# A macaron decoder trunk on one core: another order of the feed-forwards' first products, earlier convolution taps, own tiles for residual sums, a split last tile

## The chip, the cores and the metric

The kernel runs on 1 core of one Trainium2 chip. The metric is the device time of one execution in microseconds (us); where runs are compared, it is the median of several. Engines are named as in the profile: PE (TensorE, matmuls and transposes), PEld (its weight loads), DVE (VectorE), ACT (ScalarE), POOL (GpSimd), SP (SyncE, which issues nearly all DMAs).

## The reference

One layer over 1024 tokens of width 1024, in float32:

```python
x = x + 0.5 * swiglu(rms_norm(x, ffn1_norm), w_gate, w_up, w_down)      # hidden width 2816
x = x + token_mixer(rms_norm(x, mix_norm) @ w_in) @ w_out
x = x + 0.5 * swiglu(rms_norm(x, ffn2_norm), w_gate2, w_up2, w_down2)
out = rms_norm(x, final_norm)

def swiglu(h, w_gate, w_up, w_down):
    return (silu(h @ w_gate) * (h @ w_up)) @ w_down
```

The token mixer joins three parts along the channels: a pool mixer (256 channels: trailing means over 2, 4, 8 and 16 tokens minus the token, then a small matrix per group), attention with forget gates (8 heads of 64; the logits get the running sum of the log gates) and a convolution part (256 channels: a gated linear unit, a causal depthwise convolution of 31 taps, a layer norm, silu). All matrices are multiplied to float32 accuracy.

## The kernel before, in words

**Precision.** Each operand is split into a high and a low part: ACT casts the high part, DVE subtracts it to get the low part (`split`, L77). A product is then three matmuls: high by high, high by low, low by high.

**Stages.** Feed-forward 1, the mixer's input projections, attention (with the rest of the output projection as filler), the last output projection, feed-forward 2 and the final norm follow one another on PE.

**Feed-forward (L339).** Gate and up products use a Strassen scheme (Winograd's form) in place of eight block products: seven. The 1024 x 1024 input is four blocks of 512 x 512: 11, 21, 12 and 22 (the first two of rows 0 to 511). The combinations t1 = 12 - 11, t2 = 22 - t1, t3 = 22 - 12, t4 = 21 - t2 are computed by DVE in the rows' tiles (`combine`, L258); each block is turned by PE transposes, four rows' tiles in one go as `turn` (one PSUM bank) or `turn_two` (a pair of banks), and split by ACT and DVE into its own tile. On the weights' side `Pair` holds the four weight blocks of two groups of 128 hidden columns, for gate and up; sums s1 to s4 go the same way (`sum`, L297) and each is split by `prepare` (L312). There are 11 pairs (NQ). The class `Products` runs the seven products of a pair; each is 2 x 12 matmuls of 128 x 512 (`both`, L407). Products 11 and 21 add up in one PSUM pair (`pa`), t2, t3 and t4 in another (`pb`), t1 and 22 in a third (`pc`). What comes out is gated (`gated`, L359), combined and stored in DRAM for the down projection, which follows the same scheme.

**Order in the feed-forward's head.** The sequence of products (L485) takes pairs 0 and 1 together for "11" and "21", then pair 0 and pair 1 each with t2, t1, t3, 22, t4; later pairs run 11, t2, 21, t1, t3, 22, t4. Turns and combinations of the input blocks still missing are run from a list, one entry behind each half product (`steps`, L266; `both` pops them). Operands are prepared up to three products ahead (L500).

**Order in general.** The program is ordered at build time by a scheduler: the earlier in the program, the higher the priority, and an instruction whose inputs are late by the planner's clock is passed by later ones. Each engine then runs its instructions in that fixed order, and waits where one isn't ready. Where it mattered the order is pinned: `in_order` (L109) makes all instructions of an engine from a point on follow one another as written, `follow` (L122) puts one behind another. Tiles come from pools with a fixed number of slots (`g2`, 11 scratch slots; `x`, 8 row tiles, used for weights once the rows are turned; `xb`; `w`). PSUM has tag `b` with four banks and tag `a` with two pairs of banks. A tile's slot is free once its last reader, DMA or engine, is through.

**Mixer.** Gates of the convolution part (`gate`, L725), two pool projections (`pool_mm`, `pool`), values (L808), eight query/key projections (`qk`, L887). The 62 convolution taps (31 for each of two halves) are DVE instructions, dealt out by `conv(n)` (L714) between other work; `behind` makes the next tap follow a given instruction. `running_sum` (L846) turns the log gates on PE, sums them by a scan on DVE, splits the sum and stores the terms that attention reads. A projection's result sits in a pair of PSUM banks (`pp`, two of them), which `qk_out` (L899) splits and stores; so projection i needs the banks of projection i - 2.

**Last output projection (L1176).** For each tile t of 128 rows, 12 matmuls, an addition of the residual into `xs[t]`, a store of it (`kept`, read back in the down projection), the squares on ACT, GpSimd's power -1/2, and the scaling by DVE, which overwrites `xs[t]`. From t = 2 on the blocks 11 and 21 of tile t - 2 are turned.

**Final tile (`finish`, L1218).** The last 128 rows, after the last matmul: squares in two halves on ACT, their sum on DVE, power on GpSimd, two scalings on DVE, two stores from SP.

Of the kernel before, what the change touches and what calls it, by code (L numbers as in the profile page):

```python
# [18 lines left out]
P = 128  # L19
# [28 lines left out]
def trunk_kernel(  # L48
# [84 lines left out]
    class Rows:  # L133


        def __init__(self, gain):
            self.gain = load_gain(gain)
            self.xn, self.ss = {}, {}
# [12 lines left out]
        def scale(self, t):  # L151
            rs = self.inverse(t)
            nc.vector.scalar_tensor_tensor(self.xn[t], xs[t], rs, self.gain, op0=ALU.mult, op1=ALU.mult)
# [60 lines left out]
    class Operands(Rows):  # L214
# [9 lines left out]
        def square(self, t):  # L224
            self.xn[t] = xs[t]
            self.ss[t] = small.tile([P, 1], F32, name="ss")
            squares = slot("g2", F32, name="squares")
            nc.scalar.activation(squares, xs[t], AF.Square, scale=D ** -0.5, accum_out=self.ss[t])
# [37 lines left out]
        def steps(self):  # L266


            turn = lambda n, *cs: [lambda c=c: self.turn(n, c) for c in cs]
            two = lambda n, c: [lambda: self.turn_two(n, c)]  # L270
            return [
                [], turn("22", 0, 1), turn("22", 2, 3) + [lambda: self.combine("t1", "t3", "t2")], [], [],
                turn("t2", 0, 1), turn("t2", 2, 3), two("t1", 0) + [lambda: self.combine("t4")], two("t1", 2), two("t3", 0), two("t3", 2), two("t4", 0), two("t4", 2),
            ]
# [4 lines left out]
    class Pair:  # L279
# [17 lines left out]
        def sum(self, n):  # L297


            if not self.sums:  # L300
                a = self.a
                s1 = slot("g2", F32, (P, 2, 4, P), name="s")
                nc.vector.tensor_tensor(s1, a[1, 0], a[1, 1], op=ALU.add)
                nc.vector.tensor_tensor(a[1, 0], a[0, 0], a[1, 0], op=ALU.subtract)
                nc.vector.tensor_tensor(a[0, 0], s1, a[0, 0], op=ALU.subtract)
                self.sums = {"s1": s1, "s3": a[1, 0], "s2": a[0, 0]}
            if n == "s4" and n not in self.sums:
                self.sums[n] = a = self.a[0, 1]
                nc.vector.tensor_tensor(a, a, self.sums["s2"], op=ALU.subtract)
            return self.sums[n]  # L310
# [28 lines left out]
    def ffn(ws, xt, pairs, rows, more, late, after, later):  # L339
# [65 lines left out]
        begin = len(nc.cur_bb.bb.instructions)  # L405

        def both(pair, right, o, start):  # L407
            for m in range(2):
                product(o[m], pair.ops[right], right, m, start)
                if more:  # L410
                    for f in more.pop(0):
                        f()

        class Products:


            def __init__(self, pair):
                self.pair = pair
                self.A = self.B = self.C = None

# [7 lines left out]
            def p_21(self):  # L428
                A, ta = self.A, temp("ta")
                self.ta = ta  # L430
                both(self.pair, "21", A, False)
                gated(A[0], A[1], ta[:, 0], ta[:, 1])

            def p_t2(self):
                self.B = [bank(name="pb") for m in range(2)]
                self.u2 = temp("u2")
                both(self.pair, "t2", self.B, True)
# [11 lines left out]
            def p_t3(self):  # L449
# [8 lines left out]
                put(0, ta, 2)  # L458

            def p_22(self):  # L460
                C, u2, p5, ta = self.C, self.u2, self.p5, self.ta
# [3 lines left out]
                gated(u2[:, 0], u2[:, 1], u2[:, 0], u2[:, 1])  # L465

# [18 lines left out]
        early, rest = ("11", "21"), ("t2", "t1", "t3", "22", "t4")  # L485
        sequence = [(q, n) for n in early for q in range(2)] + [(q, n) for q in range(2) for n in rest]
        sequence += [(q, n) for q in range(2, NQ) for n in ORDER]
        work = {}
        for i, (q, n) in enumerate(sequence):
            if i == 4:  # L490
                pairs[1].load(1, 0), pairs[1].load(1, 1)
            if q >= 1 and n in ("11", "t2") and q + 1 == len(pairs) < NQ and i > 4:
                pairs.append(Pair(ws, q + 1))
# [3 lines left out]
            if i == 9:  # L497
                in_order(begin, DVE)

            for q2, n2 in sequence[i:i + (1, 1, 3, 3, 3, 3)[i] if i < 6 else i + 4]:  # L500
# [61 lines left out]
        in_order(begin, PE)  # L562
# [53 lines left out]
    in_order(begin, PE, DVE, ACT)  # L616
    more1 = norm1.steps()
# [78 lines left out]
    ffn(ws, operands, pairs1, x, more1, late1, after1, later1)  # L696
# [51 lines left out]
    gate(1, 0, None, lambda: conv(3))  # L748
    fetch()
    gate(1, 1, None, lambda: (conv(3), ready(2)))  # L750
# [57 lines left out]
    for j in range(2):  # L808
        wv, k = loaded[4 + j], 4 - j
        for t in range(NT):  # L810
# [34 lines left out]

    def running_sum():  # L846
# [14 lines left out]
        terms = slot("g2", F32R, name="terms")  # L861
# [47 lines left out]
    qk(2, lambda: None, running_sum)  # L909
    qk(3)  # L910
# [260 lines left out]
    for i in range(4):  # L1171
        pairs2[i // 2].load(0, i % 2)
# [3 lines left out]
    for t in range(NT):  # L1176
        ts = slice(t * P, (t + 1) * P)
        o = banks((P, 2, HALF), name="po") if t % 2 == 0 else [bank(name="po") for _ in range(2)]
        for c in range(2):
# [4 lines left out]
            if t % 2:  # L1184
                nc.vector.tensor_tensor(xs[t][:, cs], oc, xs[t][:, cs], op=ALU.add)
# [9 lines left out]
        if t in (3, 5):  # L1195
            pairs2[0].prepare(("11", "21")[t // 2 - 1])
# [3 lines left out]
    for n in ("11", "21"):  # L1200
        pairs2[1].prepare(n)
    more2 = norm2.steps()
    in_order(begin, PE, DVE)
# [14 lines left out]
    def finish():  # L1218

        r, t = last[0], NT - 1  # L1220
        xn = slot("g2", F32, name="xn")
        ss = small.tile([P, 2], F32, name="ss2", bufs=1)
        cs = [slice(c * HALF, (c + 1) * HALF) for c in range(2)]
        for c in range(2):
            nc.scalar.activation(
                xn[:, cs[c]], xs[t][:, cs[c]], AF.Square, scale=D ** -0.5, accum_out=ss[:, c:c + 1]
            )
        r.ss[t] = small.tile([P, 1], F32, name="ss")
# [6 lines left out]
    ffn(ws, norm2.tiles, pairs2, kept, more2, late2, after2, lambda t: None)  # L1235
# [33 lines left out]
```

## Time and profile before

| | |
|---|---|
| three runs | 1762.13, 1766.65, 1768.06 us (median 1766.65) |
| profiled execution | 1767.13 us; span of its instructions 1765.4 us |
| granted PE clock, mean | 0.991 of full speed |
| PE busy | 1723.7 us (98%), 8213 instructions |
| DVE busy | 1216.5 us (69%) |
| ACT busy | 690.1 us (39%) |
| POOL busy | 164.1 us (9%) |
| DMA | 209.69 MB, mean 119 GB/s |

A row of the timeline gives start and duration in us, engine, line, operation, output <- inputs, shape, the number of instructions merged, and in brackets the idle time before it and what ended that. A row of the waits gives the total of a wait in us, how often it came and the longest. A row of a table by stretch gives the busy time of each engine with its count of instructions, the granted clock (1.00 is 2.4 GHz, 0.50 is 1.2 GHz), the DMA share and GB/s. Matmuls overlap: one lasts 0.39 us, and the next starts 0.23 us after it.

### The profile page before, as it was taken

To read this page: it belongs to the slowest core of one execution; us is meant where nothing else is said; L and a number is where in the kernel's file an instruction comes from. 1 tells how busy PE (TensorE), PEld (TensorE's weight loads), DVE (VectorE), ACT (ScalarE), POOL (GpSimd) and SP (SyncE) were. 2 spreads that over 40 slices of the span, in tenths; PEclk is the share of its full clock that TensorE was granted. 3 is DMA by queue.
4 is the path that set the end of the run, shared out by engine and by line. 5 is a ranking of instruction groups with operands and counts; after the bars stand their busy time and mean duration, and the time that the engine had idled before them with its cause. 6 is when DMAs were issued, how large, how long until landed. Compare 5 with 4: busy or idle time off the path is not lost.

```text
span 1765.4 us, 21430 instructions
## 1 busy us (share of the span) xinstructions
PE 1723.7 (98%) x8213; PEld 1432.2 (81%) x8214; DVE 1216.5 (69%) x1465; ACT 690.1 (39%) x968; POOL 164.1 (9%) x218
## 2 busy tenths in 40 slices
PE   8999999999999999999899999899999999999998
PEld 6788888888888788898788887788888888888886
DVE  7766666555787674699567786876655566678676
ACT  5433333333334433222545664443333333334343
POOL 3000000000000100221134452100000000000010
PEclk9999999999999999999999999999999999999999
DMA  5333233335723323012563413252333332853342
GB/s 179 109 130 102 89 102 130 99 106 225 282 95 114 102 84 96 1 50 75 170 158 74 121 38 112 68 161 90 104 129 101 102 102 90 334 190 103 106 144 83
DMA packets 173687, 209.69 MB, mean 119 GB/s; under 512 B 9969, under 2 KB 116496, under 8 KB 173584
## 3 DMA queue, kind: packets, MB, share of 16 engines
q1 hardware_dynamic: 173584, 208.31, 36.9%
q8 instruction: 65, 1.06, 0.3%
q14 instruction: 38, 0.31, 0.1%
HBM read 150.87 MB, written 57.41 MB: 118 GB/s over the span
## 4 chain that ended last, share of the span: by engine, by line
PE 48%; DVE 7%; ACT 1%; issue 1%; DMA 1%; POOL 0%; DVEq 0%; POOLq 0%; ACTq 0%
PE pb L354 10%; PE pc L354 6%; PE pa L354 6%; PE po L529 4%; PE po L530 4%; PE po L531 4%; DVE ua L721 4%; PE ysum L1083 2%; PE ptp L1072 2%; PE po L192 1%; PE po L194 1%; PE po L193 1%; PE s L1035 1%; PE s L1036 1%; PE pp L192 1%; PE pp L193 1%
## 5 line engine op out<-in xcount | busy, mean ns | idle before, releaser
L354 PE MATMUL pb<-ot,hi 128*128 128x512 f32 x1056 | 329.9, 393 | 4.4 <-DVE ot L80 4.4
L80 DVE TENSOR_TENSOR lo<-a,hi 128x1024 fp32r<-128x1024 f32 x132 | 161.3, 1223 | 166.8 <-ACT hi L79 166.8
L529 PE MATMUL po<-dh,hh 128*128 128x512 f32 x616 | 240.6, 391 | 1.0 <-DVE x L537 1.0
L530 PE MATMUL po<-dl,hh 128*128 128x512 f32 x616 | 240.1, 390 | 0.0
L531 PE MATMUL po<-dh,hl 128*128 128x512 f32 x616 | 240.0, 390 | 0.0
L354 PEld LDWEIGHTS pb<-ot,hi 128*128 128x128 f32 x1056 | 199.7, 189 | 47.0 <-DVE ot L80 5.8
L79 ACT CAST hi<-a 128x1024 fp32r<-128x1024 f32 x132 | 139.2, 1055 | 250.3 <-PE pa L354 136.7
L354 PE MATMUL pa<-o,hi 128*128 128x512 f32 x704 | 217.7, 390 | 0.0
L354 PE MATMUL pb<-ot,lo 128*128 128x512 f32 x528 | 206.9, 392 | 0.0
L354 PEld LDWEIGHTS pa<-o,hi 128*128 128x128 f32 x704 | 131.6, 188 | 27.1
L147 POOL TENSOR_SCALAR rs<-ss 128x1 f32<-128x1 f32 x32 | 16.9, 529 | 1323.0 <-ACT xn L143 1275.5
L354 PE MATMUL pa<-o,lo 128*128 128x512 f32 x352 | 137.1, 390 | 1.6 <-DVE lo L80 1.6
L529 PEld LDWEIGHTS po<-dh,hh 128*128 128x128 f32 x616 | 116.0, 188 | 25.9 <-DVE x L537 1.8
L531 PEld LDWEIGHTS po<-dh,hl 128*128 128x128 f32 x616 | 115.9, 188 | 24.3
L79 ACT CAST dh<-ds 128x1024 fp32r<-128x1024 f32 (+1 forms) x60 | 58.9, 982 | 195.7 <-DVE ds L395 177.2
L530 PEld LDWEIGHTS po<-dl,hh 128*128 128x128 f32 x616 | 115.9, 188 | 23.8
L354 PEld LDWEIGHTS pb<-ot,lo 128*128 128x128 f32 x528 | 100.0, 189 | 20.8
L354 PE MATMUL pc<-ot,hi 128*128 128x512 f32 x352 | 108.7, 390 | 0.0
L354 PE MATMUL pc<-o,hi 128*128 128x512 f32 x352 | 108.4, 389 | 0.0
L80 DVE TENSOR_TENSOR dl<-ds,dh 128x1024 fp32r<-128x1024 f32 (+1 forms) x60 | 68.1, 1135 | 51.4 <-ACT dh L79 51.3
L80 DVE TENSOR_TENSOR hl<-hr,hh 128x1024 fp32r<-128x1024 f32 x84 | 95.0, 1131 | 2.3 <-PE po L530 0.8
L721 DVE SCALAR_TENSOR_TENSOR ua<-ua,cw 128x1023 f32<-128x1023 f32 (+29 forms) x60 | 88.3, 1491 | 0.6
(243 smaller groups left out, 3173.8 us busy)
## 6 DMA issues: line engine op xcount, KB each, us to landing
hr<-hid SPq DMA_DIRECT2D x70, 512.0 KB
a<-in_ffn_w_gate_dram SPq DMA_DIRECT2D x88, 256.0 KB
a<-in_ffn_w_up_dram SPq DMA_DIRECT2D x88, 256.0 KB
wd<-in_ffn_w_down_dram SPq DMA_DIRECT2D x8, 2048.0 KB
st<-qkd SPq DMA_DIRECT2D x48, 256.0 KB
hid<-ta SPq DMA_DIRECT2D x22, 512.0 KB
hid<-p SPq DMA_DIRECT2D x22, 512.0 KB
x<-in_x_dram SPq DMA_DIRECT2D x16, 512.0 KB
```

The costliest lines, as they stand in the source:

```text
L79: nc.scalar.copy(hi, src)
L80: nc.vector.tensor_tensor(lo, src, f32(hi), op=ALU.subtract)
L192: nc.tensor.matmul(o, wh, mh, start=(i == 0), stop=False)
L193: nc.tensor.matmul(o, wh, ml, start=False, stop=False)
L194: nc.tensor.matmul(o, wl, mh, start=False, stop=(i == n - 1))
L354: nc.tensor.matmul(o, a[:, m, k, :], r[:, b, k, :], start=(start and k == n == 0), stop=(k == 3 and n == 2), skip_group_check=not start,)
L529: nc.tensor.matmul(o[t], hh[:, k, ts], wh[:, k], start=(g == 0 and k == 0), stop=False)
L530: nc.tensor.matmul(o[t], hh[:, k, ts], wl[:, k], start=False, stop=False)
L531: nc.tensor.matmul(o[t], hl[:, k, ts], wh[:, k], start=False, stop=(g == 5 and k == n - 1))
L721: nc.vector.scalar_tensor_tensor(a[:, s:], u[:, :T - s], k, a[:, s:], op0=ALU.mult, op1=ALU.add)
L1072: nc.tensor.transpose(tp[:, k, i, :], items[head * NT + 2 * j + i][0][:, kt * P:(kt + 1) * P], ident)
L1083: nc.tensor.matmul(yp[:, j % 2, :], vs[key_tile(j, u, k)][:, head], pts[:, x % 4, s, k, :], start=(u == 0 and k == 0 and s == 0), stop=(u ...
```

## The change

1. **Sequence of the heads.** Pairs 0 and 1 still begin with 11 and 21; then come t1, t2, 22, t3, t4. t1 of pair 1 is put ahead of t4 of pair 0, and t4 of pair 1 behind 11 of pair 2. t2 is combined in t1's place (rows 0 to 511) once t1 is turned, and 22 stays where it is until it is turned. Weight sums come singly, as entries of the list.
2. **Products.** Work on a half that needs one half product only (`then`) is issued behind that half, ahead of the list's entry. What needs both 22 and t3 is done by whichever comes second (`half`).
3. **Pinned order.** DVE's order is pinned from the norm's start to product t1 of pair 1 in one piece, in both feed-forwards.
4. **Mixer.** More taps are issued in the gates (7 and 7 for 3 and 3), fewer in the pool projections (2 and 1 for 4 and 3); in the values a tap is issued behind the split. The running sum is issued behind projection 2's output, its terms in projection 3; the next taps follow the scan.
5. **Last output projection.** The residual sum goes into a scratch tile of its own, which is stored, squared (the squares into `xs[t]`) and scaled into `xs[t]`. Second weight blocks of pairs 0 and 1 are loaded behind tiles 3 and 5, and "11" of both pairs is split there; "21" of both after the loop.
6. **Final tile.** No addition on DVE: GpSimd adds the two sums and the epsilon; the first half is multiplied by the gain on DVE before the power is there and scaled on ACT, the second half is done on DVE, and the two stores go out from ACT and SP.

The diff, cut to its core:

```diff
 # Operands: rows, squares, the list
+        def square(self, t, src=None):
+            self.xn[t], self.src[t] = xs[t], xs[t] if src is None else src
+            squares = slot("g2", F32, name="squares") if src is None else xs[t]
+            nc.scalar.activation(squares, self.src[t], AF.Square, scale=D ** -0.5, accum_out=self.ss[t])
-                    "t1": (0, 0), "t4": (0, 1), "t3": (1, 0), "t2": (1, 1)}[n]
+                    "t1": (0, 0), "t2": (0, 0), "t4": (0, 1), "t3": (1, 0)}[n]
-                [], turn("22", 0, 1), turn("22", 2, 3) + [lambda: self.combine("t1", "t3", "t2")], [], [],
-                turn("t2", 0, 1), turn("t2", 2, 3), two("t1", 0) + [lambda: self.combine("t4")], two("t1", 2), two("t3", 0), two("t3", 2), two("t4", 0), two("t4", 2),
+                add("t1"), total("s1"), [], turn("t1", 0, 1), turn("t1", 2, 3) + add("t2") + total("s2"), [],
+                turn("t2", 0, 1), two("t2", 2) + total("s4"), two("22", 0), two("22", 2) + add("t3"), two("t3", 0),
+                two("t3", 2) + add("t4"), two("t4", 0), two("t4", 2),
 # ffn: products and their sequence
+        def both(pair, right, o, start, then=None):
             for m in range(2):
                 product(o[m], pair.ops[right], right, m, start)
+                if then is not None:
+                    then(m)
 # p_21
-                both(self.pair, "21", A, False)
-                gated(A[0], A[1], ta[:, 0], ta[:, 1])
+                both(self.pair, "21", A, False, lambda m: m and gated(A[0], A[1], ta[:, 0], ta[:, 1]))
 # p_t2
-                for m in range(2):
+                def then(m):
                     nc.vector.tensor_tensor(self.B[m], self.B[m], self.p1[:, m], op=ALU.add)
                     nc.scalar.copy(self.u2[:, m], self.B[m])
+                both(self.pair, "t2", self.B, True, then)
-        early, rest = ("11", "21"), ("t2", "t1", "t3", "22", "t4")
+        early, rest = ("11", "21"), ("t1", "t2", "22", "t3", "t4")
+        sequence[8:10] = sequence[9:7:-1]
+        sequence.insert(14, (1, "t4"))
-                in_order(begin, DVE)
+                in_order(first if begin is None else begin, DVE)
 # mixer
-    gate(1, 0, None, lambda: conv(3))
+    gate(1, 0, None, lambda: conv(7))
-    gate(1, 1, None, lambda: (conv(3), ready(2)))
+    gate(1, 1, None, lambda: (ready(2), conv(7)))
-    pu = pool_mm(0, lambda h: (ready(3), fetch()) if h else conv(4))
+    pu = pool_mm(0, lambda h: (ready(3), fetch()) if h else conv(2))
-    pu = pool_mm(1, lambda h: conv(3) if h else ready(4))
+    pu = pool_mm(1, lambda h: conv(1) if h else ready(4))
-            conv(1)
             split(vs[t][:, 4 * j:4 * j + 4, 0, :], vs[t][:, 4 * j:4 * j + 4, 1, :], vv)
+            conv(1)
 # running_sum, now ended by the scan; the rest is sum_terms
+        behind.update({0: last_instruction(), 1: last_instruction()})
-    qk(2, lambda: None, running_sum)
-    qk(3)
+    qk(2)
+    running_sum()
+    qk(3, lambda: None, sum_terms)
 # last output projection
-    for i in range(4):
-        pairs2[i // 2].load(0, i % 2)
+    for pair in pairs2:
+        pair.load(0, 0)
+        sums = slot("g2", F32, name="sums")
-            nc.vector.tensor_tensor(xs[t], o.rearrange("p c x -> p (c x)"), xs[t], op=ALU.add)
-        nc.sync.dma_start(kept[ts, :], xs[t])
-        norm2.square(t)
+            nc.vector.tensor_tensor(sums, o.rearrange("p c x -> p (c x)"), xs[t], op=ALU.add)
+        nc.sync.dma_start(kept[ts, :], sums)
+        norm2.square(t, sums)
         if t in (3, 5):
-            pairs2[0].prepare(("11", "21")[t // 2 - 1])
+            pairs2[t // 2 - 1].prepare("11")
+            pairs2[t // 2 - 1].load(0, 1)
-    for n in ("11", "21"):
-        pairs2[1].prepare(n)
+    for pair in pairs2:
+        pair.prepare("21")
 # finish
-        nc.vector.tensor_tensor(r.ss[t], ss[:, 0:1], ss[:, 1:2], op=ALU.add)
-        rs = r.inverse(t)
-        for c in range(2):
-            nc.vector.scalar_tensor_tensor(xn[:, cs[c]], xs[t][:, cs[c]], rs, r.gain[:, cs[c]], op0=ALU.mult, op1=ALU.mult)
-            nc.sync.dma_start(out[t * P:(t + 1) * P, cs[c]], xn[:, cs[c]])
+        nc.vector.tensor_tensor(xn[:, cs[0]], xs[t][:, cs[0]], r.gain[:, cs[0]], op=ALU.mult)
+        nc.gpsimd.tensor_scalar(rs, ss[:, 0:1], ss[:, 1:2], EPS, op0=ALU.add, op1=ALU.add)
+        nc.gpsimd.tensor_tensor(rs, rs, mhalf, op=ALU.pow)
+        nc.scalar.activation(xn[:, cs[0]], xn[:, cs[0]], AF.Copy, scale=rs)
+        nc.vector.scalar_tensor_tensor(xn[:, cs[1]], xs[t][:, cs[1]], rs, r.gain[:, cs[1]], op0=ALU.mult, op1=ALU.mult)
+        nc.scalar.dma_start(out[t * P:(t + 1) * P, cs[0]], xn[:, cs[0]])
+        nc.sync.dma_start(out[t * P:(t + 1) * P, cs[1]], xn[:, cs[1]])
```

## Rows read from the trace of the kernel before

**Rows 1.** Busy time by stretch, one of feed-forward 2's steady stretches:
```profile
1250.00:1275.00 25.00, 25.00 (x112) 20.70 (x111) 13.96 (x16) 8.15 (x12) 0.00 (x0) 1.00 0.25 76
```

**Rows 2.** The same view, four stretches behind long waits of PE:
```profile
49.10:56.20 7.10, 6.49 (x20) 4.89 (x21) 6.96 (x10) 1.01 (x1) 0.00 (x0) 0.56 0.01 2
844.70:848.70 4.00, 3.96 (x10) 3.16 (x11) 2.31 (x2) 0.74 (x1) 0.00 (x0) 0.51 0.85 266
1090.70:1094.40 3.70, 3.70 (x12) 2.92 (x11) 3.34 (x5) 1.99 (x4) 1.54 (x2) 0.54 0.34 142
1141.30:1145.50 4.20, 3.26 (x11) 2.37 (x10) 4.20 (x7) 1.01 (x1) 0.00 (x0) 0.60 0.02 4
```

**Rows 3.** Waits of PE, 20 to 90 us (head of feed-forward 1):
```profile
PE tp L252 <- DVE ta L362: 2.1, 1, 2.1
PE pb L354 <- DVE ot L80: 2.0, 2, 1.4
PE tp L233 <- DVE x L153: 1.8, 2, 1.0
```

**Rows 4.** Timeline, PE behind its first product and DVE, 24 to 41 us:
```profile
24.73 0.60 PE L233 MATMUL tp<-ident,x 128*128 128x128 f32 x4
...
29.62 1.28 DVE L153 SCALAR_TENSOR_TENSOR x<-x,rs,gb 128x1024 f32<-128x1024 f32 x1 [0.46 <-POOL rs L148]
...
33.22 2.49 DVE L264 TENSOR_TENSOR x<-x,x 128x512 f32<-128x512 f32 x4
...
40.43 1.23 DVE L303 TENSOR_TENSOR s<-a,a 128x1024 f32<-128x1024 f32 x1
```

**Rows 5.** Timeline of the projections: PE, ACT and DVE
```profile
826.25 1.03 PE L856 MATMUL lp<-ident,gates 128*8 128x128 f32 x8
...
844.74 0.76 PE L192 MATMUL pp<-xt,wh 128*128 128x512 f32 x1 [6.15 <-DVE qkl L85]
...
839.86 1.04 ACT L79 CAST terms<-fd 8x1024 fp32r<-8x1024 f32 x1 [17.27 <-DVE fd L858]
...
735.47 0.15 DVE L769 COPY pr<-pu 64x1 f32<-64x1 f32 x1 [11.13 <-ACT pu L765]
...
827.27 9.04 DVE L721 SCALAR_TENSOR_TENSOR ua<-ua,cw 128x1005 f32<-128x1005 f32 x7
```

**Rows 6.** Timeline, GpSimd's weight splits and taps of DVE beside such:
```profile
724.63 4.76 POOL L183 TENSOR_TENSOR wl<-raw,wh 128x1024 fp32r<-128x1024 f32 x2 [42.88 <-ACT wh L182]
...
774.01 4.60 DVE L721 SCALAR_TENSOR_TENSOR ua<-ua,cw 128x1021 f32<-128x1021 f32 x2
```

**Rows 7.** Timeline, into feed-forward 2: DVE and POOL (tile 0), PE
```profile
1088.54 1.28 DVE L153 SCALAR_TENSOR_TENSOR x<-x,rs,gb 128x1024 f32<-128x1024 f32 x1 [3.92 <-DMA kept<-x]
...
1084.08 0.57 POOL L148 TENSOR_TENSOR rs<-rs,mhalf 128x1 f32<-128x1 f32 x1
...
1140.49 1.06 PE L252 MATMUL tp<-ident,x 128*128 128x128 f32 x8 [2.09 <-DVE ta L362]
```

**Rows 8.** Waits of PE, 1075 to 1180 us (into feed-forward 2):
```profile
PE tp L233 <- DVE x L153: 5.1, 3, 3.3
PE pb L354 <- DVE ot L80: 2.4, 2, 1.4
PE pa L354 <- DVE lo L80: 1.6, 1, 1.6
```

**Rows 9.** Timeline, final tile: ACT, DVE, POOL; first a power beside DVE
```profile
28.19 1.40 POOL L148 TENSOR_TENSOR rs<-rs,mhalf 128x1 f32<-128x1 f32 x1
...
1759.04 0.19 ACT L1225 ACTIVATION_READ_ACCUMULATOR xn<-x 128x1 f32 x1
...
1758.69 1.28 DVE L153 SCALAR_TENSOR_TENSOR xn<-x,rs,gb 128x1024 f32<-128x1024 f32 x1 [0.21 <-POOL rs L148]
...
1761.04 1.42 DVE L1232 SCALAR_TENSOR_TENSOR xn<-x,rs,gb 128x512 f32<-128x512 f32 x2 [1.00 <-POOL rs L148]
...
1760.13 0.22 POOL L147 TENSOR_SCALAR rs<-ss 128x1 f32<-128x1 f32 x1 [1.48 <-DVE ss L1229]
```

More of the change, by code (lines that the diff above doesn't have):

```diff
@@ L297, in sum @@
         def sum(self, n):
-            if not self.sums:
-                a = self.a
-                s1 = slot("g2", F32, (P, 2, 4, P), name="s")
+            a, sums = self.a, self.sums
+            if not sums:
+                s1 = sums["s1"] = slot("g2", F32, (P, 2, 4, P), name="s")
                 nc.vector.tensor_tensor(s1, a[1, 0], a[1, 1], op=ALU.add)
+            if n != "s1" and "s2" not in sums:
+                sums["s3"], sums["s2"] = a[1, 0], a[0, 0]
                 nc.vector.tensor_tensor(a[1, 0], a[0, 0], a[1, 0], op=ALU.subtract)
[L305 to L310, printed above, removed]
+                nc.vector.tensor_tensor(a[0, 0], sums["s1"], a[0, 0], op=ALU.subtract)
+            if n == "s4" and n not in sums:
+                sums[n] = a[0, 1]
+                nc.vector.tensor_tensor(a[0, 1], a[0, 1], sums["s2"], op=ALU.subtract)
+            return sums[n]
         def prepare(self, right):
@@ L337, in trunk_kernel, with ffn @@
     PLACE = (0, 3, 6, 5, 1, 2, 4)
-    def ffn(ws, xt, pairs, rows, more, late, after, later):
+    def ffn(ws, xt, pairs, rows, more, late, after, later, begin=None):
         hid = dr.tile([7, NQ, P, HALF], F32, name="hid")
@@ L402, in ready @@
             downs[i] = *ops, n
-        begin = len(nc.cur_bb.bb.instructions)
-        def both(pair, right, o, start):
+        first = len(nc.cur_bb.bb.instructions)
+        def both(pair, right, o, start, then=None):
             for m in range(2):
                 product(o[m], pair.ops[right], right, m, start)
+                if then is not None:
+                    then(m)
                 if more:
@@ L419, in __init__ @@
                 self.A = self.B = self.C = None
+                self.halves = 0
             def p_11(self):
@@ L458, in p_t3 @@
                 put(0, ta, 2)
+                self.half()
             def p_22(self):
[L461 removed]
+                C, u2 = self.C, self.u2
                 both(self.pair, "22", C, False)
@@ L465, in p_22, with half @@
                 gated(u2[:, 0], u2[:, 1], u2[:, 0], u2[:, 1])
+                self.half()
+            def half(self):
+                self.halves += 1
+                if self.halves < 2:
+                    return
+                u2, p5, ta = self.u2, self.p5, self.ta
                 nc.vector.tensor_tensor(p5[:, 0], u2[:, 1], p5[:, 1], op=ALU.add)
@@ L482, in p_t4 @@
                 put(6, p7[:, 0:1], 1)
-        early, rest = ("11", "21"), ("t2", "t1", "t3", "22", "t4")
-        sequence = [(q, n) for n in early for q in range(2)] + [(q, n) for q in range(2) for n in rest]
-        sequence += [(q, n) for q in range(2, NQ) for n in ORDER]
+        early, rest = ("11", "21"), ("t1", "t2", "22", "t3", "t4")
+        sequence = [(q, n) for n in early for q in range(2)] + [(0, n) for n in rest]
+        sequence += [(1, n) for n in rest[:-1]] + [(q, n) for q in range(2, NQ) for n in ORDER]
+        sequence[8:10] = sequence[9:7:-1]
+        sequence.insert(14, (1, "t4"))
         work = {}
@@ L491, in ffn @@
                 pairs[1].load(1, 0), pairs[1].load(1, 1)
-            if q >= 1 and n in ("11", "t2") and q + 1 == len(pairs) < NQ and i > 4:
+            if q >= 1 and n in ("11", "t1") and q + 1 == len(pairs) < NQ and i > 4:
                 pairs.append(Pair(ws, q + 1))
@@ L561, in ffn @@
                 add(t)
-        in_order(begin, PE)
+        in_order(first, PE)
     ws = ffn1_w_gate[0], ffn1_w_up[0], ffn1_w_down[0]
@@ L615, in trunk_kernel @@
     rows_of(7)
-    in_order(begin, PE, DVE, ACT)
-    more1 = norm1.steps()
+    in_order(begin, PE, ACT)
+    begin1 = begin
+    more1 = norm1.steps(pairs1[0])
     operands = norm1.tiles
@@ L694, in later1 @@
         mix[0].flip(t, 4)
-    ffn(ws, operands, pairs1, x, more1, late1, after1, later1)
+    ffn(ws, operands, pairs1, x, more1, late1, after1, later1, begin1)
     norm = mix[0]
@@ L844, in log_sigmoid @@
         nc.vector.scalar_tensor_tensor(a, a, 0.0, b, op0=ALU.min, op1=ALU.subtract)
+    sums = {}
     def running_sum():
@@ L860, in running_sum, with sum_terms @@
             )
-        terms = slot("g2", F32R, name="terms")
+        behind.update({0: last_instruction(), 1: last_instruction()})
+        sums["fd"] = fd
+    def sum_terms():
+        fd, terms = sums["fd"], slot("g2", F32R, name="terms")
         fh, fl, nh, nl = (terms[32 * i:32 * i + HEADS, :] for i in range(4))
@@ L1199, in trunk_kernel @@
         pairs2[0].load(1, j)
-    for n in ("11", "21"):
-        pairs2[1].prepare(n)
-    more2 = norm2.steps()
-    in_order(begin, PE, DVE)
+    for pair in pairs2:
+        pair.prepare("21")
+    more2 = norm2.steps(pairs2[0])
+    in_order(begin, PE)
     last = []
```

26 lines of the change are left out of this document (12 added, 14 removed).

## The prediction

> **What bounds the kernel now.** I read the busy times by stretch first. Inside the feed-forwards' steady stretches TensorE (PE) is full: 25.0 of 25 us with 112 matmuls, so 5.4 us for a product of 24, while VectorE (DVE) works 14.0 of 25 [rows 1]. No part of the change shortens a matmul, and the number of matmuls and transposes stays, so nothing is to be had there. What can be had lies where PE waits or runs at the lower clock. The waits of PE, taken once over each of three stretches, and the granted clock behind them give it: the head of feed-forward 1, the middle of the query/key projections, and the passage from the last output projection into feed-forward 2. In each, PE waits for a DVE that works through a queue in a fixed order, and a long wait is followed by a stretch at about half the clock (0.51 to 0.60 granted, the lower of the two levels for most of it) [rows 2]. What follows the last matmul is the fourth place.
>
> **Feed-forward 1, head.** Before: PE waits 1.8 us for the scaling of rows 4 to 7 (it turns block 22 between the two "11" products), 2.1 for the gate product that must free a PSUM pair, 2.0 for late splits [rows 3], and 49.1 to 56.2 us runs at clock 0.56: 0.44 of 6.5 busy us, 2.9 [rows 2]. Sum 8.8. The 2.1 comes from DVE's queue: behind the last scaling stand twelve combinations (three groups of 2.5 us) and three weight sums of 1.23, the first sum only at 40.43, and the gate product behind them [rows 4]. After: no turn between the "11" products; the first ended at 24.73 [rows 4], so the second ends at 30.2. DVE ends the last scaling at 30.9 and needs 0.62 for each t1 piece (a quarter of 2.49): the first turn of t1 starts at 31.5, the second piece comes at 32.1. That wait is 1.5. Then DVE has t1's other pieces, one sum, four splits, t2's four combinations, two sums: 2.5 + 1.2 + 2 x 1.3 + 1.2 + 2.5 + 2.5 = 12.5 from 30.9, plus the gate product's 0.7, so 44.1; PE asks for the freed pair after its fourth product, at about 45.2. Margin 1.1, wait gone. What is late next: t3 is combined behind the second split of 22 and t4 behind that of t3, each just when PE arrives; by the same count 0.5 each. The first weight sum of pair 1 needs its loads; they start when block t3's first turn frees two slots, some 8 us before DVE is there. The products of the second pair's t1 need a PSUM pair that product 22's two additions free, by the count 1 us ahead. New waits 1.5 + 1.1 = 2.6, none as long as the ones that a lower clock followed. Gain 6.2. Bounds: 8.8 (no wait left) and -3 (DVE 2 us later than counted at the gate product and at pair 1's t1, each with the clock's 2.9).
>
> **Projections.** Before: PE waits 6.15 us [rows 5], then 844.7 to 848.7 at 0.51, 2.0 more [rows 2]; 8.1 in all. The chain: the PSUM pair of projection 2 must be split before projection 4 may start. ACT's half of that split stands behind the cast of the running sum, for which ACT waits 17.3 us; the sum's scan starts on DVE at 836.2, behind seven convolution taps that take 9.04 us from 827.27, when its input was there [rows 5]. After: the running sum is issued behind projection 2's split, its terms a projection later, and taps that come later in the program wait for the scan. The split then follows projection 2 at once, about 10 us before it is needed, and projection 3's weight loads no longer stand behind the terms' stores on SP's queue. Four more taps precede the values, and of 16 instead of 10 before the first pooling six fall into DVE's idle 11.1 us at 724 [rows 5]; GpSimd's 4.8 us of work there stretches them (a pair of taps took 4.6 where 2.6 is usual [rows 6]), so 6 x 1.29 + 4 = 11.7 us, which fits but for 0.6. DVE is 7 us ahead from there on. It needs that lead: about eleven taps can't run until the scan is done at about 830, then 11 x 1.25, the terms' low part, projection 3's low part and two splits of 1.3 end at about 849 to 851, while PE wants them for the channel means at 849.2. I take a wait of 1.5 (0 to 4.5 with a fall of the clock). Splits of the values ahead of the taps: no wait of PE stands there today, 0. Gain 8.1 - 1.5 = 6.6; bounds 8.1 and 0.
>
> **Into feed-forward 2.** Before: scaling tile 0 overwrites the residual rows while their store is under way: DVE idles 3.9 us for that DMA, though the inverse root was done at 1084.65 [rows 7]; tile 7 waits in the same way. PE waits 5.1 for scaled rows (3.3 the longest), 1.6 for a weight split behind tile 7, then as in feed-forward 1 2.1 and 2.4 [rows 7, 8]: 11.2, and at clock 0.54 and 0.60 [rows 2] 0.46 x 3.7 + 0.40 x 3.3 = 3.0. Sum 14.2. After: the sum is written to a tile of its own, stored from there and scaled into xs; scaling 0 ends at 1086.0, before PE's first turn (1086.6). The other turns stay bound by DVE's round of an addition, two splits and a scaling (3.8 us with 1.2 twice for a weight split) against PE's 3.6: waits of 0.3, 0.3 and 1.4. Squares go into xs instead of a scratch tile: the number of scratch tiles is the same, but each is held until its store has landed. Two of the four weight loads leave SP's queue ahead of the first store and come between later stores; if a slot isn't free there, the stores behind it wait too, and tile 7's slot with them. PE doesn't need tile 7 before t1's turn, 10.9 us behind its last projection; DVE gets to t1's first piece 10.7 behind it. Then as in feed-forward 1, t3 and t4 0.55 each. New waits 3.1, gain 11.1; bounds 14.2 and 3 (tile 7 and both long waits again).
>
> **End.** Before, from the last square's accumulator (1759.23) [rows 9] an addition on DVE (hidden: DVE was busy with tile 6 until 1759.97), GpSimd's 0.22 + 0.57, two scalings of 0.7 in a row that end at 1762.46. After: no addition, the first half multiplied by the gain early, then scaled on ACT (0.6, an estimate from its square of that size) beside DVE's second half, with a store from each queue. GpSimd alone would end at 1760.1, the outputs at 1760.9: gain 1.5. Beside a busy DVE the same power took 1.40 instead of 0.57 [rows 7, 9]; twice so, 1762.7: -0.3. DVE is busy with tile 6 for half of it [rows 9]: 1761.6, gain 0.8.
> By the Trainium skill (SBUF — State Buffer, "Who interferes with whom"), a DVE instruction with two SBUF inputs and a GpSimd one that reads SBUF exclude each other for a whole instruction. This speaks against starting GpSimd sooner, under tile 6's scaling, and against the added multiplication; by the rule the end gains nothing and the time below would be 1743.2. The row of 1.40 agrees with it.
>
> **The steady products** keep their order; DVE's and ACT's steps on t2's first half now stand between its halves. Cover: 11 of 25 us in which DVE is idle [rows 1]. Cost 0; without the cover, see the last rival.
>
> **Sum.** The profiled execution took 1767.13 us, 1.7 of it outside the span of 1765.4; the median of the three runs is 1766.65, the same within 0.03%. 1767.1 - 6.2 - 6.6 - 11.1 - 0.8 = 1742.4.
>
> **Rivals.**
> 1. DVE becomes the bound of the heads. For: the margins counted (1.1, 1.0, 0.2 us) are small, and from the scaling to pair 1's t1 the order of DVE is now one fixed queue. Against: DVE's work in the heads doesn't grow, only its order changes. Then each head keeps one wait of 2.1 with its 2.9 of low clock, and the means wait 4.5: 1742.4 + 10 + 3 = 1755.4.
> 2. The counted waits vanish too (the heads and the means find DVE early): 2.6 + 1.5 + 3.1 less, 1735.2. Against: the scaling that t1 needs isn't moved.
> 3. The change doesn't do what it says: the waits come back at the next instruction in the same length, since DVE has the same work before the same product; 1767. Against: the 6.15 and the two waits for stores hang on an order and on a buffer, not on DVE's work.
> 4. Slower: in each of the nine steady pairs of a feed-forward PE comes to wait, since t2's addition and copy now stand ahead of operand splits on DVE and ACT. With the head's 2.1 each time, 18 x 2.1 = 38: 1780. It decides from 24.7 / 18 = 1.4 us a pair. Against: the 11 idle us, and operands that are split three products (16 us) ahead.
>
> **Chances.** Forecast 0.60, rival 1 0.22, rival 2 0.08, rival 3 0.04, rival 4 0.06. A run can tell 0.3% (5 us) from no change. Forecast and rivals 1 and 2 lie beyond it: faster 0.90; same 0.04; slower 0.06. The range takes in rivals 1 and 2 with a little beyond them: 1733 to 1758.
>
> **What would show it.** Right: no PE wait on a query/key projection and a scan right behind its transposes; no DVE wait on a store of the residual; a first t1 turn about 1.5 us late; granted clock 1.0 around 50, 845, 1091 and 1142 (of the old count). Wrong in a step: PE waits for the gate product, for pair 1's t1, or over 2 us for the means. Wrong as a whole: waits of PE inside the steady products, or fewer than 112 matmuls in 25 us there.

## The result, and the profile after

The changed kernel takes 1737.3 us (median of 4 runs, 1736.78 to 1738.44) beside 1767.18 for the kernel before (4 runs). The ratio of the runs is 0.9838 (95% interval 0.9818 to 0.9857; it is not the quotient of the two medians). The forecast was 1742.4 with a range of 1733 to 1758. The profiled execution took 1738.44 with a span of 1736.7, so the two profiled executions differ by 28.7 us. Where these lie is read from the starts of the same PE instructions in both traces:

| stretch on PE | before | after | gain | forecast |
|---|---|---|---|---|
| first product to first down-projection, feed-forward 1 | 438.0 | 431.0 | 7.0 | 6.2 |
| from there to the first query/key projection | 333.7 | 332.9 | 0.8 | 0 |
| first to last matmul of the query/key projections | 102.5 | 94.0 | 8.5 | 6.6 |
| from there to the last logits | 167.8 | 167.7 | 0.1 | 0 |
| last logits to the last product 11 of feed-forward 2 | 463.9 | 451.1 | 12.8 | 11.1 |
| from there to the last matmul | 232.3 | 232.3 | 0 | 0 |
| last matmul to the end of the span | 8.1 | 8.5 | -0.4 | 0.8 |

The waits of PE, 20 to 90 us after, where [rows 3] had 5.9 us:

```profile
PE tp L235 <- DVE x L266: 1.3, 1, 1.3
PE tp L254 <- DVE x L266: 0.6, 2, 0.3
```

The same view, 1055 to 1185 us, where [rows 8] had 9.1 and [rows 7] 2.1:

```profile
PE tp L235 <- DVE x L154: 1.1, 2, 0.9
PE tp L254 <- DVE x L266: 0.6, 2, 0.3
```

In the projections no wait of more than 0.3 us is left. The scan on DVE and the cast on ACT, which waited 17.27 us in [rows 5]:

```profile
820.92 1.20 DVE L883 TENSOR_TENSOR_SCAN fd<-one,lp 8x512 f32<-8x512 f32 x1
...
823.58 1.05 ACT L79 CAST terms<-fd 8x1024 fp32r<-8x1024 f32 x1 [3.83 <-DVE fd L883]
```

Busy time by stretch, at the places that answer to [rows 2] and, last, to [rows 1] (columns: PE, PEld, DVE, ACT, POOL, granted clock, DMA):

```profile
45.70:52.80 7.10, 7.10 (x42) 6.03 (x40) 4.87 (x7) 4.78 (x6) 0.00 (x0) 1.00 0.01 3
830.00:838.00 8.00, 8.00 (x37) 6.62 (x36) 7.96 (x6) 3.47 (x4) 2.23 (x2) 1.00 0.64 200
1068.00:1073.00 5.00, 5.00 (x28) 4.23 (x27) 4.24 (x6) 3.27 (x6) 1.11 (x3) 1.00 0.44 179
1112.00:1116.00 4.00, 4.00 (x23) 3.40 (x22) 3.36 (x5) 2.19 (x3) 0.00 (x0) 1.00 0.01 2
...
1225.00:1250.00 25.00, 25.00 (x112) 20.70 (x111) 16.01 (x19) 8.60 (x12) 0.00 (x0) 1.00 0.20 64
```

PE is busy all through and the clock is 1.00 in each; the steady stretch has its 112 matmuls as before.

### The profile page after: what moved, and what is told of

Read it like the earlier page. It is cut to its first block, busy times and chain, and to the rows that moved or that the text cites. A ratio compares the mean times of both kernels' runs of the same rounds, so it can differ in the third digit from the quotient of the medians.

```text
span 1736.7 us, 21426 instructions
## 1 busy us (share of the span) xinstructions
PE 1714.3 (99%) x8213; PEld 1425.4 (82%) x8214; DVE 1222.8 (70%) x1462; ACT 691.3 (40%) x967; POOL 170.4 (10%) x218
## 4 chain that ended last, share of the span: by engine, by line
PE 93%; DVE 2%; POOL 1%; ACT 1%; issue 1%; DMA 1%; SPq 0%; POOLq 0%; DVEq 0%; ACTq 0%
PE pb L360 20%; PE pc L360 13%; PE pa L360 13%; PE po L551 8%; PE po L552 8%; PE po L553 8%; PE ysum L1113 2%; PE pp L193 2%; PE pp L195 2%; PE pp L194 2%; PE ptp L1102 2%; PE po L193 2%; PE po L195 2%; PE po L194 2%; PE s L1065 1%
## 5 line engine op out<-in xcount | busy, mean ns | idle before, releaser
L360 PE MATMUL pb<-ot,hi 128*128 128x512 f32 x1056 | 325.7, 390 | 0.0
L744 DVE SCALAR_TENSOR_TENSOR ua<-ua,cw 128x1023 f32<-128x1023 f32 (+29 forms) x60 | 95.5, 1609 | 0.7
```

The costliest lines, as they stand in the source:

```text
L360: nc.tensor.matmul(o, a[:, m, k, :], r[:, b, k, :], start=(start and k == n == 0), stop=(k == 3 and n == 2), skip_group_check=not start,)
L744: nc.vector.scalar_tensor_tensor(a[:, s:], u[:, :T - s], k, a[:, s:], op0=ALU.mult, op1=ALU.add)
```

## The experiments

All times are medians, and each ratio is to the kernel before; the stretches are those of the table, read from one profiled execution of each kernel. The diffs are cut to what tells the experiments apart.

**Feed-forward 1 in the order of before** (sequence, list, `then` and DVE's pin of the kernel before, for this feed-forward alone):

```diff
-    norm1 = Operands(ffn1_norm)
+    norm1 = Operands(ffn1_norm, True)      # old list, t2 in 22's place
-    ffn(ws, operands, pairs1, x, more1, late1, after1, later1, begin1)
+    ffn(ws, operands, pairs1, x, more1, late1, after1, later1, begin1, True)
```

> The changed kernel, with feed-forward 1's first products back in the order of the kernel before (block 22 turned between the two 11 products, t2 first). Theory (the head's order is worth its own term, and the parts add up): the two traces put the first matmul of feed-forward 1's down-projections at 457.1 us before and 450.2 after, so 1737.3 + 6.9 = 1744.2, with the waits of 1.8, 2.1 and 2.0 us and the stretch at the lower clock behind 49 us back. If the 0.8 us that were gained at the entry of the mixer (a stretch of 3.4 us at the lower clock from 616 us in the trace of before, none after) hang on this order too, 1745.0 and that stretch is seen again. Rival (DVE has the same work before the same products, so the head's gain came from elsewhere): 1737 to 1739.

Measured: 1743.55 (ratio 0.987, 0.9855 to 0.9884). The stretch takes 435.0 us, 4.0 more than after and 3.0 less than before. Waits of PE, 20 to 90 us, and the stretch behind them:

```profile
PE pb L369 <- DVE ot L80: 2.4, 2, 1.4
PE tp L257 <- DVE ta L377: 2.1, 1, 2.1
PE tp L236 <- DVE x L154: 1.2, 2, 0.8
```

```profile
50.00:56.00 6.00, 5.06 (x27) 4.25 (x27) 6.00 (x9) 1.88 (x2) 0.00 (x0) 1.00 0.01 3
```

The waits are back, 5.7 us against 1.9, which is the 4.0 nearly whole. The lower clock that followed the same waits before (0.56, [rows 2]) did not come in this execution; the spans of the four executions go from 1740.8 to 1742.9 at mean clocks of 0.998 to 0.996. So the order is worth 4 us, and the clock's 2.9 only where it falls; that it fell in the longer of these executions is likely, but they were not traced. The place at 616 us kept its clock too.

**Mixer as before** (all of part 4 of the change undone):

> The changed kernel, with the whole mixer part undone (taps as before, ahead of the values' splits; running sum and its terms between projection 2's half and its split). Theory (the gain of 8.5 us between the first and the last projection in the two traces belongs to this part alone): 1737.3 + 8.5 = 1745.8; ACT idles some 17 us for the sum's cast, PE waits about 6 us in projection 4 and runs some 4 us at the lower clock behind it. Rival (DVE's later work sets it, not the order): 1737 to 1740, with the wait at the channel means instead.

Measured: 1747.58 (0.9891, 0.9875 to 0.9908). First to last projection 102.3 us, 8.3 more; ACT waits 17.17 us for the sum's cast. PE:

```profile
837.85 0.76 PE L193 MATMUL pp<-xt,wh 128*128 128x512 f32 x1 [6.14 <-DVE qkl L85]
```

The whole gain of the projections belongs to this part. Here the fall of the clock at the mixer's entry is back (0.79 from 608 to 616 us), though the instructions ahead of it stand as in the kernel after.

**The two halves of that part.** Only the running sum back, the taps' places as after. With it goes the line that makes the next taps follow the scan (left out of the cut):

```diff
-    qk(2)
-    running_sum()
-    qk(3, lambda: None, sum_terms)
+    qk(2, lambda: None, running_sum)
+    qk(3)
```

> The changed kernel, with only the running sum and its terms back between projection 2's first half and its split; the taps stay early and behind the values' splits. Theory 1 (the place of the sum is the cause, as forecast: ACT's half of projection 2's split stands behind the sum's cast): the split is late again and PE waits in projection 4, up to 6 us and 2.9 of lower clock behind it, 1743 to 1746. Theory 2 (the lead is the cause: six taps went into DVE's idle time, the scan comes some 7 us sooner, more than the 6.15 of the wait): 1737 to 1739.

Measured: 1746.67 (0.9889, 0.9874 to 0.9903), projections 101.8 us. PE waits 5.9 us in all, 2.24 at projection 3 and 3.61 at projection 4. The latter, then ACT and DVE:

```profile
836.60 0.47 PE L193 MATMUL pp<-xt,wh 128*128 128x512 f32 x1 [3.61 <-DVE qkl L85]
...
832.90 1.04 ACT L79 CAST terms<-fd 8x1024 fp32r<-8x1024 f32 x1 [16.35 <-DVE fd L883]
...
821.65 7.71 DVE L744 SCALAR_TENSOR_TENSOR ua<-ua,cw 128x1000 f32<-128x1000 f32 x6
829.28 1.20 DVE L883 TENSOR_TENSOR_SCAN fd<-one,lp 8x512 f32<-8x512 f32 x1
```

The scan starts at 829.28, as with the mixer as before (829.34). The lead of the early taps is not used: DVE fills it with taps from further down, and the scan still stands behind six of them. And only the taps back, the sum as after:

```diff
-    gate(1, 0, None, lambda: conv(7))
+    gate(1, 0, None, lambda: conv(3))
...
-            split(vs[t][:, 4 * j:4 * j + 4, 0, :], vs[t][:, 4 * j:4 * j + 4, 1, :], vv)
             conv(1)
+            split(vs[t][:, 4 * j:4 * j + 4, 0, :], vs[t][:, 4 * j:4 * j + 4, 1, :], vv)
```

> The changed kernel, with only the taps back (fewer ahead of the first pooling, and ahead of the values' splits); the running sum stays behind projection 2's split. Theory 1 (the place of the sum alone takes the wait away): no wait in projection 4, but DVE is some 7 us later at the channel means, for which PE then waits 4 to 6 us with up to 2 of lower clock: 1741 to 1745. Theory 2 (PE finds other work there, or DVE catches up): 1737 to 1739.

Measured: 1738.79 (0.9845, 0.983 to 0.9859), which can't be told from after; projections 93.9 us, no PE wait over 0.3. The cause is the place of the sum together with the taps held behind its scan; these two were not run apart. The taps' new places are worth nothing that shows.

**Into feed-forward 2: the order.** The second feed-forward in the order of before, with the sums' own tiles:

> The changed kernel, with feed-forward 2's first products in the order of the kernel before; the sums keep tiles of their own. Theory (the passage's gain of 12.8 us in the traces is 4.8 for the sums' tiles and 8.0 for the order): 1737.3 + 8.0 = 1745.3, with the waits for block 22's rows, for the gate product (2.1) and for late splits (2.4) back and a stretch at the lower clock behind them. Rival (the waits were those of the stores, so that the order is worth little once the stores are out of the way): 1737 to 1740.

Measured: 1743.76 (0.9869, 0.9854 to 0.9884); the stretch takes 456.7, 5.5 more. PE, and the clock behind:

```profile
1116.57 1.06 PE L257 MATMUL tp<-ident,x 128*128 128x128 f32 x8 [2.09 <-DVE ta L377]
1118.81 0.79 PE L369 MATMUL pb<-ot,hi 128*128 128x512 f32 x1 [0.94 <-DVE ot L80]
```

```profile
1118.00:1124.00 6.00, 5.19 (x20) 4.29 (x21) 6.00 (x9) 0.68 (x1) 0.00 (x0) 0.72 0.01 3
```

**Into feed-forward 2: stores.** The change moved three things here: the sums into tiles of their own, two of four weight loads behind stores, and the split of pair 1's "11" weights ahead of tile 7's scaling. The first two are undone, each alone and both together; the third was not.

```diff
 # sums_old
-        sums = slot("g2", F32, name="sums")
+        sums = xs[t]
-        norm2.square(t, sums)
+        norm2.square(t)
 # loads_old
     for pair in pairs2:
-        pair.load(0, 0)
+        pair.load(0, 0), pair.load(0, 1)
-            pairs2[t // 2 - 1].load(0, 1)
```

> The changed kernel, with the residual sums of the last output projection written into xs again, stored from xs and scaled over it. Theory (the store that is under way holds the first scaling back, and no other wait of that passage hangs on it): DVE idles about 3.9 us for the DMA at the first scaling, PE's first turn waits about 3.3 us and then runs 3.7 us at about half the clock: 3.3 - 0.2 + 1.7 = 4.8, so 1742.1. Rival 1 (tile 7's store comes late as well, and t1's turn needs tile 7): 3 us and a second stretch at the lower clock more, 1746 to 1747. Rival 2 (the new order of the products gives DVE enough room to take the wait): 1737 to 1738.

> The changed kernel, with the four weight loads of feed-forward 2's first two pairs ahead of the first store of a sum again, as before; the sums keep tiles of their own. Theory 1 (the wait at the first scaling was the store's landing time behind those loads, and either a tile of its own or an early store takes it away): 1737 to 1738, no DVE wait at the first scaling, though the first store lands late. Theory 2 (what counts is when the stores go out): the sums' tiles come free late and an addition waits for one: 3 to 5 us more, 1740 to 1742.

> The changed kernel, with both undone: the four loads ahead of the first store, and the sums written into xs, stored from it and scaled over it. Theory 1 (either one is enough, so with neither the wait is back): DVE idles about 3.9 us for the DMA at the first scaling, PE's first turn waits about 3.3 us and runs 3.7 us at about half the clock: 1737.3 + 3.1 + 1.7 = 1742.1. Theory 3 (the new order of the products alone took the wait away, whatever the stores do): 1737 to 1738.5, as with the sums in xs alone (1738.55).

| | time | ratio to before | stretch, against after |
|---|---|---|---|
| sums into xs | 1738.55 | 0.9841 (0.9826 to 0.9855) | +0.8 |
| four loads first | 1740.49 | 0.9852 (0.9835 to 0.9868) | +3.4 |
| both | 1742.7 | 0.9865 (0.9851 to 0.988) | +4.7 |

In the profiled executions of all three, attention, which lies ahead of this stretch, is 1.2 to 1.5 us shorter than after (last section).

GpSimd's power and DVE's first scaling, which needs it, with the sums in xs alone; then that scaling with both:

```profile
1066.16 0.57 POOL L148 TENSOR_TENSOR rs<-rs,mhalf 128x1 f32<-128x1 f32 x1
...
1068.11 1.29 DVE L154 SCALAR_TENSOR_TENSOR x<-x,rs,gb 128x1024 f32<-128x1024 f32 x1 [1.33 <-ACT squares L230]
```

```profile
1071.83 1.28 DVE L154 SCALAR_TENSOR_TENSOR x<-x,rs,gb 128x1024 f32<-128x1024 f32 x1 [3.95 <-DMA kept<-x]
```

With the sums in xs alone the row names ACT's squares, but those of this tile were done at 1065.77 and the power at 1066.73. The store, issued at 1064.61, landed at 1067.90 by its semaphore in the trace: this scaling waits for the store too, 1.3 us where the kernel before had 3.9. Tile 7's scaling waits 1.6 for its store, and PE 0.7 at its first turn. SP in the kernel with both, where the first store of a sum stands behind eight transfers:

```profile
1063.63 0.46 SPq L300 DMA_DIRECT2D a<-in_ffn_w_gate_dram  x1
1064.13 0.60 SPq L300 DMA_DIRECT2D a<-in_ffn_w_up_dram  x1
1065.72 30.05 SPq L1219 DMA_DIRECT2D kept<-x  x8
```

With the four loads first and own tiles the wait only moves to the next addition, which needs a slot that a store still holds:

```profile
1067.58 1.29 DVE L154 SCALAR_TENSOR_TENSOR x<-sums,rs,gb 128x1024 f32<-128x1024 f32 x1
1072.41 1.22 DVE L1218 TENSOR_TENSOR sums<-po,x 128x1024 f32<-128x1024 f32 x1 [3.54 <-DMA kept<-sums]
```

So theory 2 of the run with four loads first holds: what counts is when the stores land. With two loads ahead the first store lands 3.3 us past its issue, and overwriting the rows costs 0.8; with four ahead it lands 6.0 past its issue, and a tile of its own saves only 1.3 of the 4.7.

**The end.** The last tile as before; the multiplication behind the last addition; and behind the scaling of tile 6 as well:

```diff
 # mul_late; mul_last adds a second follow, behind the scaling of tile 6
         nc.vector.tensor_tensor(xn[:, cs[0]], xs[t][:, cs[0]], r.gain[:, cs[0]], op=ALU.mult)
+        mul = nc.cur_bb.bb.instructions
+        follow(mul[-1], next(i for i in mul[-2::-1] if i.engine == DVE))
```

> The changed kernel, with the last tile's scaling as before (both halves on DVE one after the other, the two sums of squares added on DVE, both stores from one queue). What is read is the time from the start of the last matmul to the end of the span: 8.1 us in the trace of before, 8.5 after. Theory (the trace of after: the new end is slower): 8.1 again, 1736.9 in all. Rival (the forecast's term: the new end is worth 0.8, and what the trace shows is scatter): 9.3, 1738.1.

> The changed kernel, with the added multiplication of the last tile's first half placed behind the last addition on DVE. Time from the start of the last matmul to the end of the span (8.5 us after): theory (the multiplication cost its 0.5 us of delay of the last addition): 8.0. Rival (what ends last is GpSimd's power chain, which waits for DVE's scaling of tile 6, and that only trades places with the multiplication): 8.4 to 8.5.

> The changed kernel, with the multiplication behind the scaling of tile 6 as well, in DVE's idle time ahead of the last scaling. Counted from the start of the last matmul, addition 0.5 to 1.1, scaling of tile 6 from 1.45 to 2.75, last sum of squares at 2.0. If GpSimd's first instruction is held until DVE's scaling has ended (as the 0.76 us in the trace of after suggest): power done at 3.6, last scaling at 3.65 instead of 4.07, so 8.1 us in all, and a total of 1736.9. If it is not held: power done at 2.9, last scaling behind the multiplication at 3.4, 7.85 in all. If the end doesn't hang on this order: 8.5.

From the last matmul's start to the end of the span: 8.0 with the old end (1738.06; 0.9844, 0.9829 to 0.9858), 8.2 with the multiplication late (1736.92, one run; that it is 1.5 below after's profiled execution is due to attention, see the last section), 8.3 with it last (1737.63; 0.9841, 0.9827 to 0.9856), 8.5 after. The times can't be told from one another here; the traces can. After:

```profile
1728.70 0.68 DVE L1260 TENSOR_TENSOR xn<-x,gb 128x512 f32<-128x512 f32 x1
1729.31 0.68 DVE L559 TENSOR_TENSOR x<-po,x 128x512 f32<-128x512 f32 x1
...
1730.15 1.28 DVE L154 SCALAR_TENSOR_TENSOR xn<-x,rs,gb 128x1024 f32<-128x1024 f32 x1 [0.16 <-POOL rs L148]
...
1730.85 0.76 POOL L1262 TENSOR_SCALAR rs<-ss 128x1 f32<-128x1 f32 x1 [0.73 <-ACT squares L1257]
...
1732.28 0.75 DVE L1265 SCALAR_TENSOR_TENSOR xn<-x,rs,gb 128x512 f32<-128x512 f32 x1 [0.84 <-POOL rs L1263]
1733.03 0.40 ACTq L1266 DMA_DIRECT2D out_dram<-xn  x1
1733.06 0.33 SPq L1267 DMA_DIRECT2D out_dram<-xn  x1
```

With the multiplication last:

```profile
1729.81 1.28 DVE L154 SCALAR_TENSOR_TENSOR xn<-x,rs,gb 128x1024 f32<-128x1024 f32 x1 [0.21 <-POOL rs L148]
...
1730.46 1.32 POOL L1264 TENSOR_SCALAR rs<-ss 128x1 f32<-128x1 f32 x1 [0.69 <-ACT squares L1257]
1731.02 0.68 DVE L1260 TENSOR_TENSOR xn<-x,gb 128x512 f32<-128x512 f32 x1
```

The old end:

```profile
1732.14 1.42 DVE L1264 SCALAR_TENSOR_TENSOR xn<-x,rs,gb 128x512 f32<-128x512 f32 x2 [0.99 <-POOL rs L148]
1732.92 0.99 SPq L1265 DMA_DIRECT2D out_dram<-xn  x2
```

Two things stand against the new end. GpSimd's first instruction takes 0.22 us alone [rows 9]; beside DVE it took 0.76, 1.10 (multiplication late) and 1.32, and ended 0.18, 0.16 and 0.08 behind the DVE instruction it ran beside, the scaling of tile 6 the first two times, the multiplication the last. So starting it sooner gave nothing. The multiplication holds GpSimd up once more: beside it the instruction ahead of tile 6's power takes 0.78 us (1728.69) where the old end has 0.22, and tile 6's scaling starts 1.9 us behind the last matmul's start, in the old end 1.4. By the Trainium skill (SBUF — State Buffer, "Who interferes with whom") a DVE instruction with two SBUF inputs keeps GpSimd from reading SBUF for its whole length; the three rows agree. And the stores: the last scaling ends 4.82 us behind the last matmul's start (5.17 before, 5.15 in the old end), but from there to the end of the span it is 3.6 (2.9, 2.9). Two stores of 256 KB issued side by side take longer to land (2.7 us from issue, where the old end's row has 2.1), and both start only when both halves are done. By the Trainium skill (DMA: Bandwidth & Descriptors, "Issuing engines are not separate DMA queues") a second issuing engine saves only the issue; the 2.7 agrees.

**t2's addition and copy behind both halves again, in every pair:**

```diff
-                both(self.pair, "t2", self.B, True, then)
+                both(self.pair, "t2", self.B, True)
+                then(0), then(1)
```

> The changed kernel, with t2's addition and copy behind both halves of the product again, in all eleven pairs of each feed-forward. Theory (the forecast's cost of 0: DVE idles 11 of 25 us there): 1737.3, within 1 us. Rival (the step between the halves is part of the gain, since it frees t2's bank sooner): 1739 to 1743, with waits of PE in the steady products.

Measured: 1739.2 (0.9849, 0.9833 to 0.9866): 1.9 above after between the medians, 0.7 between the profiled spans. The traces put 0.4 into each feed-forward's stretch, both times at the same two matmuls of its head; kernels that leave a feed-forward alone repeat its stretch within 0.1. In feed-forward 1 the first of the two starts when a weight split on DVE has ended:

```profile
86.35 0.50 PE L360 MATMUL pb<-ot,lo 128*128 128x512 f32 x1
...
85.08 1.22 DVE L80 TENSOR_TENSOR lo<-a,hi 128x1024 fp32r<-128x1024 f32 x1
```

PE has no wait in the steady products. The step between the halves costs nothing there, as forecast, and gains 0.9 in the heads, which no term of the sum had.

## Why the prediction was right, step by step

- **The bound** was read rightly: PE's waits and the clock behind them, at the heads, the projections and the passage; the steady products gave nothing, either way.
- **Feed-forward 1, head** (forecast 6.2, measured 7.0). The first turn of t1 waits 1.3 (counted 1.5), t3 and t4 0.3 each (0.5), and the gate product runs at 42.85 (44.1 counted), so its wait is gone. Both terms are borne out, but the experiment shows them to be of two kinds: 4.0 for waits, and 2.9 for a fall of the clock that need not come. The lower bound of -3 doesn't follow from its terms: 2 us late, less the margins of 1.1 and 1.0, and twice 2.9 of clock give -1.5.
- **Projections** (6.6, measured 8.5). The mechanism was the one forecast: scan right behind the split, at 820.92, and ACT's cast after 3.8 us of waiting in place of 17.3. The mis-sized term is the wait of 1.5 at the channel means; the rest above the bound of 8.1 is clock, 2.3 behind the wait (8.5 less 6.15) where I had counted 2.0. I had DVE's taps end at 849 to 851 and PE wait for all of it; in fact PE takes the means in two groups, at 841.2 and 846.5, with projection 5 between them, and waits for neither. Even the old taps, eight of which run from 837.84 for 12.45 us, brought no wait. That DVE needed a lead from the early taps was wrong: with the old taps' places the projections take the same time.
- **Into feed-forward 2** (11.1, measured 12.8). Waits of 1.7 instead of 3.1 are left, the largest 0.9 at the fourth turn. The sum came out, but the step "the sum is written to a tile of its own" got a credit that belongs elsewhere: the loads taken from ahead of the first store do most of it, and I had counted them only as a risk. With 4.7 for stores and 5.5 for the order, 2.6 of the 12.8 are in none of these runs. Two of PE's waits in the kernel before, 0.91 and 1.61 us, come back in none of them. PE's rows, and between them DVE's scaling of tile 7:

```profile
1099.88 1.09 PE L233 MATMUL tp<-ident,x 128*128 128x128 f32 x8 [0.91 <-DVE x L153]
...
1117.09 1.28 DVE L153 SCALAR_TENSOR_TENSOR x<-x,rs,gb 128x1024 f32<-128x1024 f32 x1 [2.38 <-DMA kept<-x]
...
1119.56 0.50 PE L354 MATMUL pa<-o,lo 128*128 128x512 f32 x1 [1.61 <-DVE lo L80]
```

  The 1.61 is for the split of pair 1's "11" weights, which stood behind that scaling and its store. The change took away the late store and moved the split, and the old place of the split was not run, nor the old order with the old stores; so which of them the 2.6 belong to stays open.
- **End** (0.8, measured -0.4). The one term with the wrong sign. I let GpSimd's duration grow to its doubled power at worst and gave half of the gain; it is held until DVE is through, the multiplication delays the last addition by 0.6, and the stores' landing, which I had left out of the sum, grew by 0.7.
- **Mixer's entry** (0, measured 0.8) was in no step: a stretch at the lower clock that the profiled execution of before has and that of after hasn't. This part of the gain is luck: the kernel with four loads first has the same instructions up to there and the lower clock.

The rest between forecast and result, 4.0 us between the profiled executions, is 0.8 + 0.8 + 1.9 + 1.7 less 1.2 for the end. The result lies nearer to the second rival (the counted waits vanish too, 1735.2, chance 0.08) than to the forecast, 2.1 against 5.1 us. Of its 7.2 us of counted waits half is gone: the one at the means vanished, those of the heads shrank to 1.9 and 1.7. So the places and causes of the gain were forecast, and the size of what would be left was put too high. DVE did not become the bound, and no wait appeared in the steady pairs.

## What to carry to other kernels

When a write waits for a store of the same tile, look first at what stands ahead of that store on its queue: moving two loads did more (3.9 of 4.7 us) than a second buffer (1.3), and with the queue full the buffer only handed the wait to the next user of its slot. An engine's early work buys a later instruction nothing while the fixed order still puts filler in front of it; move the instruction. At the end of a kernel count to the landing of the last byte, not to the last instruction.

## What the runs showed of the chip

The same waits do not always bring the lower clock. At the mixer's entry PE waits 1.0 us twice, 1 us of transposes apart, in all kernels. After, and with the four loads first (the same order of instructions up to there), PE:

```profile
607.19 1.09 PE L169 MATMUL tp<-ident,xn 128*128 128x128 f32 x8 [1.03 <-DVE xn L154]
609.24 1.09 PE L169 MATMUL tp<-ident,xn 128*128 128x128 f32 x8 [0.96 <-DVE xn L154]
```

```profile
607.14 1.09 PE L169 MATMUL tp<-ident,xn 128*128 128x128 f32 x8 [1.03 <-DVE xn L154]
609.19 1.96 PE L169 MATMUL tp<-ident,xn 128*128 128x128 f32 x8 [0.96 <-DVE xn L154]
```

In the second the transposes take 1.96 us for 1.09, and the granted clock from 606 to 612 is 0.77 instead of 1.00. The waits of 2.1 and 0.9 in a head went with the lower clock in feed-forward 2 (0.72) and without it in feed-forward 1 (1.00). Near the end of attention PE waits 0.5, 0.7 and 0.9 us within 3 us in all kernels; from 988 to 998 us the granted clock is 0.83 after and 1.00 in the kernel with the multiplication late, which has the same instructions up to there, and attention is 1.5 us shorter in the latter. The six waits of 2.97 to 6.15 us in these traces, though, were all followed by the lower clock. A forecast can take the length of a wait from a row; behind the shorter ones the clock is a chance, worth 1 to 3 us each time here, and differences of that size between single executions are not to be given to an edit.
